# W_down's products of two groups added up in the same banks, sums spread over VectorE, single banks in the tail

## The chip, the cores and the metric

The kernel runs on one core of a Trainium2 chip. The time is that of the device in microseconds (us); what is compared is the median of several runs of the same program. A matmul here is of 128x128 against 128x512.

## The reference

One decoder layer on x of 1024 tokens by 1024 columns, float32. It has a mixer (two groups of heads), and then a multilayer perceptron between two norms:

```
x = x + rms_norm(mix @ w_out, norm_mix_post)
h = rms_norm(x, norm_ffn_pre)
f = square(relu(h @ w_up))              # 1024 x 4096
x = x + rms_norm(f @ w_down, norm_ffn_post)
```

The change lies in the perceptron, but for one small helper that also serves the norms of the mixer.

## The kernel before, in words

Every product is done in three matmuls: an operand is split into a high part (a cast on ScalarE) and a low part (the rest, a subtraction on another engine), and high x high, high x low and low x high are added in PSUM (`mm3`). `split(h, l, src, eng)` does it; without `eng` the low part goes to GpSimd.

Both products of the perceptron are done in a scheme of seven products in place of eight (after Strassen and Winograd): sums of quarters of h and of W are formed first, and seven products of such sums give the quarters of the result.

The stages in order: the mixer in two halves (to about 440 us), ordered by a scheduler that simulates the engines. Then the **early pairs** (`early_pair`, banks `pe`, 16 pairs of row blocks of W_up, to 548 us), with the sums of h's quarters (`raw12`, `raw22`, `raw_t3` and the split blocks t1 to t4) as one piece of code between pair 5 and pair 6. From here the order of TensorE is that of the code. Then the **pair loop** (banks `puB`, `puC`, `puD`, to 774 us), which writes squares and their sums to memory (`fsp`, `fpl`). Then **W_down** (banks `pd`): 7 groups, each with 7 products of 24 matmuls, and for each product a piece of f (`fr`, loaded, then split into `f0`, `f1`) and a piece of W (`wr` loaded, `wt` sums, split into `whd`, `wld`); each product is flushed by one add on VectorE into one of seven accumulators `acc1` to `acc7` of 128x2048. Group 7, the last, is done without the scheme in the **tail** (banks `pl`): 8 tiles of 128 tokens, two halves of 512 columns, 12 matmuls a half; VectorE adds the accumulator, ScalarE sums the squares, GpSimd multiplies by the norm's weight, VectorE computes the root in a chain of small instructions (`rstd_steps`) and finishes with one multiply and add, and the output is written.

Loads of W and f are issued on SyncE's queue, loads of W_up for the pair loop on ScalarE's. All instructions of the four engines are recorded by one helper (line 72), so lines don't tell them apart; the names of the tiles do.

## Time and profile before

| | us |
|---|---|
| median of 3 runs | 1132.75 (1127.96 to 1136.23) |
| the profiled execution | 1130.96 |
| its span | 1129.2 |
| TensorE busy, share of the span | 1043.9, 92% |
| VectorE | 814.9, 72% |
| ScalarE | 499.4, 44% |
| GpSimd | 446.0, 39% |

The span goes from the first to the last instruction of the profiled execution; its mean granted clock of TensorE is 0.974 of the full one. An engine's share is a mean over stages that have different limits, so that the stages are read one by one below.

### The profile page before, as it was taken

The page shows a single profiled execution, that of the slowest core. Times are in us where ns is not written, and L with a number is a line of the kernel's source. Part 1 is how long each engine was busy: PE and PEld are TensorE (multiplying, and loading weights), DVE is VectorE, ACT ScalarE, POOL GpSimd, SP SyncE. Part 2 cuts the span into 40 slices and gives each one's busy share as a digit, 9 for nine tenths or more (in the row PEclk, how much of TensorE's full clock was granted, in tenths as well). Part 3 has the DMA queues.
Part 4 walks back from the last instruction along what each step waited for, and adds up shares of the span by engine and source line. Part 5 has one row for each costly group of instructions (what it writes and reads, how often), then busy time and mean ns, then how long its engine had stood idle before and what let it go on. Part 6 is the DMA issues. An engine that isn't in the chain of part 4 may idle for free.

```text
span 1129.2 us, 13208 instructions
## 1 busy us (share of the span) xinstructions
PE 1043.9 (92%) x4735; PEld 843.7 (75%) x4735; DVE 814.9 (72%) x1273; ACT 499.4 (44%) x672; POOL 446.0 (39%) x214
## 2 busy tenths in 40 slices
PE   4998999999899999977999999998999999998885
PEld 3876787777688787766777888886888888886663
DVE  6547986369985737384467777776389889989787
ACT  4547454444635434644334444444743333332221
POOL 4453426324353433493011111113544444357833
PEclk9999999999899999988999999998999999999898
DMA  6434312327542225735767666773445434632132
GB/s 206 113 108 135 131 57 80 126 75 224 172 150 70 94 75 161 241 104 161 257 223 224 223 223 224 226 246 137 147 168 172 150 126 168 235 122 72 56 121 102
DMA packets 139657, 172.41 MB, mean 153 GB/s; under 512 B 8404, under 2 KB 83272, under 8 KB 139592
## 3 DMA queue, kind: packets, MB, share of 16 engines
q1 hardware_dynamic: 105160, 152.70, 40.8%
q10 hardware_dynamic: 34432, 18.88, 5.7%
...
## 4 chain that ended last, share of the span: by engine, by line
PE 63%; DVE 19%; DMA 6%; issue 5%; ACT 3%; POOL 2%; SPq 1%; DVEq 0%; ACTq 0%; POOLq 0%
PE pd L72 21%; PE pso L72 7%; PE puB L72 6%; PE puC L72 5%; PE pl L72 4%; PE pe L72 4%; PE puD L72 3%; DVE acc L72 3%; PE psz L72 2%; PE psv L72 2%; DVE gg L72 2%; DVE v L72 2%; DMA wu<-in_w_up_dram 2%; DVE rr L72 2%; DVE xg L72 2%
## 5 line engine op out<-in xcount | busy, mean ns | idle before, releaser
L72 POOL TENSOR_TENSOR wl<-ws,wh 128x1024 fp32r<-128x1024 f32 x72 | 180.0, 2506 | 237.8 <-ACT wh L72 237.7
L72 PE MATMUL pd<-whd,f 128*128 128x512 f32 x784 | 246.3, 395 | 9.8 <-DVE acc L72 5.4
L72 POOL TENSOR_TENSOR f<-fr,f 128x1024 fp32r<-128x1024 f32 x49 | 124.7, 2548 | 153.9 <-ACT f L72 153.7
L72 PEld LDWEIGHTS pd<-whd,f 128*128 128x128 f32 x784 | 149.5, 191 | 43.7 <-ACT whdl L72 5.7
L72 PE MATMUL pd<-wld,f 128*128 128x512 f32 x392 | 154.7, 395 | 0.0
L72 ACT CAST f<-fr 128x1024 fp32r<-128x1024 f32 x49 | 51.5, 1054 | 147.2 <-PE pd L72 123.6
L72 POOL TENSOR_TENSOR wlb<-sa,whb 128x1024 fp32r<-128x1024 f32 x16 | 38.4, 2401 | 186.8 <-ACT whb L72 154.1
L72 ACT CAST wh<-ws 128x1024 fp32r<-128x1024 f32 x72 | 75.4, 1047 | 75.2 <-issue 14.7
L72 DVE TENSOR_TENSOR acc<-pd,acc 128x2048 f32<-128x2048 f32 x41 | 93.7, 2286 | 15.9 <-PE pd L72 15.7
L72 PEld LDWEIGHTS pd<-wld,f 128*128 128x128 f32 x392 | 74.9, 191 | 15.6
L72 ACT ACTIVATE u<-u 128x512 f32<-128x512 f32 (+1 forms) x66 | 44.3, 672 | 62.4 <-DVE u L72 57.1
L72 DVE TENSOR_TENSOR wld<-wt,whd 128x1024 fp32r<-128x1024 f32 x28 | 56.6, 2026 | 16.2 <-ACT whd L72 16.2
L72 PE MATMUL pe<-hTh,wh 128*128 128x512 f32 x128 | 53.0, 414 | 15.2 <-ACT s1e L72 13.0
L72 PE MATMUL pe<-hTl,wh 128*128 128x512 f32 x128 | 51.9, 406 | 0.0
L72 PE MATMUL pe<-hTh,wl 128*128 128x512 f32 x128 | 51.7, 404 | 0.0
...
L72 DVE TENSOR_TENSOR wld<-wr,whd 128x1024 fp32r<-128x1024 f32 x21 | 40.5, 1929 | 9.8 <-ACT whd L72 9.7
L72 DVE TENSOR_SCALAR gg<-gg,acs 128x128 f32<-128x128 f32 x64 | 29.7, 523 | 21.4 <-DMA gg<-acd 21.4
L72 DVE TENSOR_TENSOR u<-puB,s 128x512 f32<-128x512 f32 x32 | 22.1, 691 | 30.7 <-DMA s<-early 19.6
L72 PEld LDWEIGHTS pe<-hTh,wh 128*128 128x128 f32 x128 | 25.3, 198 | 22.4 <-ACT s1e L72 14.1
L72 DVE TENSOR_TENSOR sa<-wu 128x512 f32<-128x512 f32 x16 | 11.1, 692 | 41.2 <-DMA wu<-in_w_up_dram 41.2
L72 PE MATMUL pl<-whdl,f0l 128*128 128x512 f32 x64 | 27.9, 436 | 13.0 <-DVE acc L72 13.0
...
## 6 DMA issues: line engine op xcount, KB each, us to landing
...
```

Source lines behind the costliest of these rows:

```text
L72: ins = fn(*a, **k)
```

## The change

Four things are done. The chain of a root, for one column, uses one-input instructions with two values from memory in place of two-input ones. The sums of h's quarters become a generator that the early pairs from the sixth on draw step by step, all of it on VectorE, and with it the low parts of the weights of these pairs. W_down takes its first six groups as (0), (1, 2), (3, 4), (5, 6): the products of two groups are added up in the same banks before one flush, product 2 goes on in the banks of product 1 after its flush, and 3 in those of 5; the order is 1, 5, 2, 3, 6, 7, 4; the final sums of accumulators all lie on VectorE. The raw tiles of W are cut in other pieces with a third buffer, and the first two pieces of f use the buffers of the weights of the pair loop. The tail has eight banks of 512 columns instead of two tiles of four banks; its tiles form pairs for the root, but for the last two; the rest of x is loaded in two pieces, and the steps of chains and finishes are drawn between adds.

```diff
         else:
-            dve.scalar_tensor_tensor(v, ss, 0.5 / n, base, op0=ALU.mult, op1=ALU.add)
+            dve.tensor_scalar(v, ss, 0.5 / n, base, op0=ALU.mult, op1=ALU.add)
         yield
         dve.tensor_scalar(ti, v.bitcast(I32), 1, None, op0=ALU.logical_shift_right)
         yield
@@ -152,12 +153,15 @@
         for _ in range(3):
             yield
             if w == 1:
-                dve.scalar_tensor_tensor(t, v, r, r, op0=ALU.mult, op1=ALU.mult)
+                dve.tensor_scalar(t, r, r, v, op0=ALU.mult, op1=ALU.mult)
             else:
                 dve.tensor_mul(t, v, r)
                 dve.tensor_mul(t, t, r)
             yield
-            dve.scalar_tensor_tensor(r, t, 1.5, r, op0=ALU.subtract, op1=ALU.mult)
+            if w == 1:
+                dve.tensor_scalar(r, t, 1.5, r, op0=ALU.subtract, op1=ALU.mult)
+            else:
+                dve.scalar_tensor_tensor(r, t, 1.5, r, op0=ALU.subtract, op1=ALU.mult)
...
-    def next_unit(ahead=2):
+    def next_unit(ahead=2, eng=None):
         i = state["use"]
         state["use"] += 1
         while state["load"] < min(i + 1 + ahead, len(units)):
-            load_unit()
+            load_unit(eng)
         return ready[i]
...
-        wh, wl = next_unit()
+        wh, wl = next_unit(2, dve if p >= N_TG else pool)
...
-    for hf in range(2):
-        cs = slice(hf * 256, (hf + 1) * 256)
-        r12, r22, r3 = raw12[:, :, cs], raw22[:, :, cs], raw_t3[:, :, cs]
-        hs = {k: (v[0][:, :, cs], v[1][:, :, cs]) for k, v in B.items()}
-        sub(pool, r3, r22, r12)
-        for y in hs["b11"]:
-            sub(dve, r12, r12, f(y))
-        sub(dve, r22, r22, r12)
-        split(*hs["t2"], r22, dve)
-        split(*hs["t1"], r12)
-        split(*hs["t3"], r3)
-        for y in hs["b21"]:
-            sub(dve, r22, r22, f(y))
-    B["t4"] = t8(fpool, "tmp", "t4h"), t8(tpool, "raw", "t4l", F32R, 2)
-    split(*B["t4"], raw22, dve)
+    def t_blocks():
+
+        for hf in range(2):
+            cs = slice(hf * 256, (hf + 1) * 256)
+            r12, r22, r3 = raw12[:, :, cs], raw22[:, :, cs], raw_t3[:, :, cs]
+            hs = {k: (v[0][:, :, cs], v[1][:, :, cs]) for k, v in B.items()}
+            sub(dve, r3, r22, r12)
+            sub(dve, r12, r12, f(hs["b11"][0]))
+            yield
+            sub(dve, r12, r12, f(hs["b11"][1]))
+            sub(dve, r22, r22, r12)
+            yield
+            split(*hs["t2"], r22, dve)
+            yield
+            split(*hs["t1"], r12, dve)
+            yield
+            split(*hs["t3"], r3, dve)
+            for y in hs["b21"]:
+                sub(dve, r22, r22, f(y))
+            yield
+        B["t4"] = t8(fpool, "tmp", "t4h"), t8(tpool, "raw", "t4l", F32R, 2)
+        split(*B["t4"], raw22, dve)
+
+    sums = t_blocks()
     for p in range(N_TG, N_PAIR):
+        next(sums, None)
         nxt = early_pair(p)
         rest()
         rest = nxt
+    for _ in sums:
+        pass
...
+    SG = [(0,), (1, 2), (3, 4), (5, 6), (last,)]
+    sg_of = {g: (n, gs.index(g)) for n, gs in enumerate(SG) for g in gs}
+    ORD = (1, 5, 2, 3, 6, 7, 4)
+    MORE = {2: 1, 3: 5}
...
+    def raw_tile(n):
+
+        if n not in raws:
+            tag = (hT_tag + ("wr",))[n % 3]
+            raws[n] = (hpool if n % 3 < 2 else dpool).tile([P, 8, 512], F32, tag=tag, bufs=1, name=f"wr{n}")
+        return raws[n]
+
+    def rows(g, h):
+        n, gi = sg_of[g]
+        return raw_tile(2 * n + h)[:, 4 * gi:4 * gi + 4, :].rearrange("p (r c) n -> p r c n", r=2)
+
+    def w_load(n, h, gs=None):
+        for g in gs or SG[n]:
+            for r in range(2):
+                d = nc.sync.dma_start(rows(g, h)[:, r], downs[4 * g + 2 * r + h][1])
+                wr_loads.append(d.ins.name)
...
-            t_ = dpool.tile([P, 2, 512], F32, tag="wt", bufs=3, name=f"w{key}_{g}")
+            t_ = a_ if key == "t4" else dpool.tile([P, 2, 512], F32, tag="wt", bufs=4, name=f"w{key}_{g}")
...
-        fh = f_piece(f"{g}_{i}")
+        fh = f_piece(f"{g}_{i}", None if len(pcs) < N_CARRY else ("fh", "fl"))
...
-    def flush(g, i, ps):
+    def flush(n, i, ps):
         a_ = accs
-        if g == 0:
+        if n == 0:
             act.copy(a_[i], ps)
-        elif g == last - 1 and i == 4:
+            return
+        if n == len(SG) - 2 and i == 4:
             sub(dve, a_[4], a_[4], ps)
-        else:
-            add(dve, a_[i], ps, a_[i])
-        if g < last - 1:
             return
-        if i == 1:
+        add(dve, a_[i], ps, a_[i])
+        if n < len(SG) - 2:
+            return
+        if i == 6:
             add(dve, a_[6], a_[6], a_[1])
-            add(pool, a_[2], a_[2], a_[1])
-        elif i == 6:
+            add(dve, a_[3], a_[3], a_[6])
+        elif i == 7:
             add(dve, a_[7], a_[7], a_[6])
-        elif i == 7:
-            sub(pool, a_[4], a_[7], a_[4])
-        elif i == 5:
-            add(dve, a_[6], a_[6], a_[5])
-            add(dve, a_[3], a_[3], a_[6])
-            add(pool, a_[7], a_[7], a_[5])
-
-    w_raw(0, (0, 2))
+            sub(dve, a_[4], a_[7], a_[4])
+            add(dve, a_[5], a_[5], a_[7])
...
-        ps = psum2.tile([P, 4, 512], F32, tag="pd", bufs=2, name=f"pd{g}_{i}")
+        if g == gs[0]:
+            banks[i] = banks[MORE[i]] if i in MORE else \
+                psum2.tile([P, 4, 512], F32, tag="pd", bufs=2, name=f"pd{n}_{i}")
+        ps = banks[i]
         for t in range(4):
             tsl = slice(t * P, (t + 1) * P)
             for q in range(2):
-                mm3(ps[:, t, :], fh[:, q, tsl], fl[:, q, tsl], h[:, q, :], l[:, q, :], q == 0, q == 1)
-        flush(g, i, ps)
-    for n in range(len(seq) + 2, len(preps)):
-        if n + 1 < len(preps):
-            floads[n + 1]()
-        preps[n]()
+                mm3(ps[:, t, :], fh[:, q, tsl], fl[:, q, tsl], h[:, q, :], l[:, q, :],
+                    g == gs[0] and q == 0 and i not in MORE, g == gs[-1] and q == 1,
+                    skip_group_check=i in MORE)
+        if g == gs[-1]:
+            flush(n, i, ps)
...
+    for t in range(8):
+        if t % 4 == 0:
+            xq4 = raw_tile(2 * len(SG) + t // 4)
+            after_w(nc.sync.dma_start(xq4.rearrange("p (t c) n -> p t (c n)", c=2),
+                                      x2d[t * P:(t + 4) * P, :].rearrange("(t p) d -> p t d", p=P)))
+        xqs.append(xq4[:, 2 * (t % 4):2 * (t % 4) + 2, :].rearrange("p c n -> p (c n)"))
     dve.held = True
-    for t in range(8):
-        xqs.append(now["tok"].tile([P, D], F32, tag="tok", bufs=4, name=f"xq{t}"))
-        after_w(nc.sync.dma_start(xqs[t], x2d[t * P:(t + 1) * P, :]))
-        ss = const.tile([P, 2], F32, tag="ss2", bufs=8, name=f"ssy{t}")
-        ps = psum2.tile([P, 4, 512], F32, tag="pd", bufs=2, name=f"pl{t}")
-        tsl = slice(t * P, (t + 1) * P)
-        for dh in range(2):
-            ds_ = slice(dh * 512, (dh + 1) * 512)
-            a_ = acc(t, dh)
-            if t and dh == 0:
-                advance(t - 1, 4)
-            for j in range(4):
-                mm3(ps[:, dh, :], ffs[j][0][:, tsl], ffs[j][1][:, tsl], us[j][0][:, dh, :],
-                    us[j][1][:, dh, :], j == 0, j == 3)
-            add(dve, a_, ps[:, dh, :], a_)
-            junk = now["tok"].tile([P, 512], BF16, tag="junk", bufs=1, name=f"yj{t}{dh}")
-            act.activation(junk, a_, AF.Square, accum_out=ss[:, dh:dh + 1])
-            pool.tensor_tensor(a_, a_, wfpost[:, ds_], op=ALU.mult)
-            if dh == 0:
-                if t:
-                    advance(t - 1, 9)
-                    finish(t - 1, 1)
-                base = rstd_base(ss[:, 0:1], D)
-            elif t:
-                finish(t - 1, 0)
-        steps.append(rstd_steps(ss[:, 1:2], D, base))
-        rs.append(next(steps[t]))
-    advance(7, 9)
-    finish(7, 0)
-    finish(7, 1)
+    for ts in TAIL:
+        ss = sss[ts] = const.tile([P, len(ts), 2], F32, tag=f"st{len(ts)}", bufs=4, name=f"ssy{ts[0]}")
+        for j, t in enumerate(ts):
+            tsl = slice(t * P, (t + 1) * P)
+            for dh in range(2):
+                ds_ = slice(dh * 512, (dh + 1) * 512)
+                a_ = acc(t, dh)
+                ps = psum3.tile([P, 512], F32, tag="pl", bufs=8, name=f"pl{t}{dh}")
+                for i in range(4):
+                    mm3(ps, ffs[i][0][:, tsl], ffs[i][1][:, tsl], us[i][0][:, dh, :],
+                        us[i][1][:, dh, :], i == 0, i == 3)
+                add(dve, a_, ps, a_)
+                junk = now["tok"].tile([P, 512], BF16, tag="junk", bufs=1, name=f"yj{t}{dh}")
+                act.activation(junk, a_, AF.Square, accum_out=ss[:, j, dh:dh + 1])
+                pool.tensor_tensor(a_, a_, wfpost[:, ds_], op=ALU.mult)
+                some(6 if len(ts) > 1 else 12)
+        todo.append(chain_op(ts))
+        for t in ts:
+            todo += [finish_op(t, 0), finish_op(t, 1)]
+    some(1000)
```

The order changes as follows. First VectorE at the early pairs, before: the sums of h's quarters (`raw12`, `raw22`, against the split blocks `hTh`, `hTl`) and the low part of t2, in one run.

```order
L72 TENSOR_TENSOR b22l_3496<-tg3_1_4202,b22h_3495 128x4x128
L72 TENSOR_TENSOR raw12_3497<-raw12_3497,hTh_105 128x4x256
L72 TENSOR_TENSOR raw12_3497<-raw12_3497,hTl_106 128x4x256
L72 TENSOR_TENSOR raw12_3497<-raw12_3497,hTh_105 128x4x256
L72 TENSOR_TENSOR raw22_3498<-raw22_3498,raw12_3497 128x4x256
L72 TENSOR_TENSOR raw12_3497<-raw12_3497,hTl_106 128x4x256
L72 TENSOR_TENSOR raw22_3498<-raw22_3498,raw12_3497 128x4x256
L72 TENSOR_TENSOR t2l_4217<-raw22_3498,t2h_4216 128x4x256
L72 TENSOR_TENSOR raw22_3498<-raw22_3498,hTh_105 128x4x256
L72 TENSOR_TENSOR t2l_4217<-raw22_3498,t2h_4216 128x4x256
L72 TENSOR_TENSOR raw22_3498<-raw22_3498,hTl_106 128x4x256
```

And now, at the same place, where `wl66` to `wl68` are low parts of the weights of early pairs:

```order
L73 TENSOR_TENSOR wl66_4308<-ws66_4305,wh66_4307 128x1024
L73 TENSOR_TENSOR raw_t3_4222<-raw22_3498,raw12_3497 128x4x256 x2
L73 TENSOR_TENSOR raw12_3497<-raw12_3497,hTh_105 128x4x256
L73 TENSOR_TENSOR t3l_4221<-raw_t3_4222,t3h_4220 128x4x256
L73 TENSOR_TENSOR raw12_3497<-raw12_3497,hTh_105 128x4x256
L73 TENSOR_TENSOR t3l_4221<-raw_t3_4222,t3h_4220 128x4x256
L73 TENSOR_TENSOR raw12_3497<-raw12_3497,hTl_106 128x4x256
L73 TENSOR_TENSOR wl67_4348<-ws67_4345,wh67_4347 128x1024
L73 TENSOR_TENSOR raw12_3497<-raw12_3497,hTl_106 128x4x256
L73 TENSOR_TENSOR raw22_3498<-raw22_3498,raw12_3497 128x4x256
L73 TENSOR_TENSOR t1l_4219<-raw12_3497,t1h_4218 128x4x256
L73 TENSOR_TENSOR wl68_4390<-ws68_4387,wh68_4389 128x1024
```

The weights' low parts and those of t3 and t1 are new on VectorE and stand between the sums, which come in other turns; GpSimd has no instruction between the last weight of the early pairs that it still splits and the first of the pair loop.

Then ScalarE at the entry into W_down, before: squares of the pair loop's last sums (`u2_15`, `u3_15`), and the cast of the first f piece, `f00_1`, behind them.

```order
L72 ACTIVATE f22_15_6408<-f22_15_6408 128x512 x2
L912 DMA fpl_3936<-f22_15_6408 128x512
L72 ACTIVATE u3_15_6407<-u3_15_6407 128x512 x2
L912 DMA fpl_3936<-u3_15_6407 128x512
L72 ACTIVATE u2_15_6365<-u2_15_6365 128x512 x2
L912 DMA fpl_3936<-u2_15_6365 128x512
L72 CAST f00_1_6484<-fr0_1_6478 128x1024
L72 CAST f00_2_6494<-fr0_2_6482 128x1024
```

And now the same cast, `whf0_1`, in a buffer of the weights:

```order
L73 CAST whd15_6346<-wu31_6281 128x512
L73 ACTIVATE u2_13_6135<-u2_13_6135 128x512 x2
L73 ACTIVATE f22_14_6304<-f22_14_6304 128x512 x2
L73 CAST whf0_1_6485<-fr0_1_6478 128x1024
L916 DMA fpl_3936<-f22_14_6304 128x512
L73 ACTIVATE u3_14_6303<-u3_14_6303 128x512 x2
L916 DMA fpl_3936<-u3_14_6303 128x512
L73 CAST whd0_1_6489<-wr0_6475 128x1024
L73 CAST whf0_5_6495<-fr0_5_6483 128x1024
L73 ACTIVATE u2_14_6250<-u2_14_6250 128x512 x2
```

It stands ahead of the squares of pair 14 and of all of pair 15.

Last VectorE at the end of W_down, before: flushes (`acc<-pd,acc`), sums of accumulators (`acc<-acc,acc`) and low parts of W (`wld`).

```order
L72 TENSOR_TENSOR acc7_6474<-acc7_6474,acc6_6473 128x2048
L72 TENSOR_TENSOR acc7_6474<-pd6_7_8188,acc7_6474 128x2048
L72 TENSOR_TENSOR wldl0_8295<-wr7_8173,whdl0_8294 128x1024
L72 TENSOR_TENSOR acc5_6472<-pd6_5_8225,acc5_6472 128x2048
L72 TENSOR_TENSOR wldl1_8331<-wr7_8173,whdl1_8330 128x1024
L72 TENSOR_TENSOR acc6_6473<-acc6_6473,acc5_6472 128x2048
L72 TENSOR_TENSOR acc2_6469<-pd6_2_8266,acc2_6469 128x2048
L72 TENSOR_TENSOR acc3_6470<-acc3_6470,acc6_6473 128x2048
L72 TENSOR_TENSOR wldl2_8367<-wr7_8173,whdl2_8366 128x1024
L72 TENSOR_TENSOR acc3_6470<-pd6_3_8302,acc3_6470 128x2048
L72 TENSOR_TENSOR wldl3_8375<-wr7_8173,whdl3_8374 128x1024
L72 TENSOR_TENSOR acc4_6471<-acc4_6471,pd6_4_8338 128x2048
```

And now:

```order
L73 TENSOR_TENSOR acc6_6473<-pd3_6_8095,acc6_6473 128x2048
L73 TENSOR_TENSOR wldl0_8240<-wr8_7868,whdl0_8239 128x1024
L73 TENSOR_TENSOR acc6_6473<-acc6_6473,acc1_6468 128x2048
L73 TENSOR_TENSOR acc3_6470<-acc3_6470,acc6_6473 128x2048
L73 TENSOR_TENSOR wldl1_8275<-wr9_8195,whdl1_8274 128x1024
L73 TENSOR_TENSOR acc7_6474<-pd3_7_8170,acc7_6474 128x2048
L73 TENSOR_TENSOR wldl2_8310<-wr8_7868,whdl2_8309 128x1024
L73 TENSOR_TENSOR acc7_6474<-acc7_6474,acc6_6473 128x2048
L73 TENSOR_TENSOR acc4_6471<-acc7_6474,acc4_6471 128x2048
L73 TENSOR_TENSOR acc5_6472<-acc5_6472,acc7_6474 128x2048
L73 TENSOR_TENSOR wldl3_8318<-wr9_8195,whdl3_8317 128x1024
L73 TENSOR_TENSOR acc4_6471<-acc4_6471,pd3_4_8247 128x2048
```

Five flushes stand in the rows before and three in those of now. Of the sums of accumulators four were on VectorE and three on GpSimd; now there are five, all on VectorE, three of them in a row ahead of the last low part of W and the last flush.

## Rows read from the trace of the kernel before

**Rows 1.** Busy time by stage: start:end, length, then each engine, clock, DMA.
```profile
core 0: us, PE busy (x) PEld busy (x) DVE busy (x) ACT busy (x) POOL busy (x), PEclk, DMA share, GB/s
28.00:484.00 456.00, 434.82 (x2158) 351.49 (x2157) 301.72 (x747) 225.66 (x327) 191.91 (x103) 0.98 0.40 126
484.00:525.00 41.00, 28.03 (x99) 22.04 (x99) 32.89 (x13) 19.33 (x26) 27.27 (x10) 0.83 0.37 117
498.30:501.00 2.70, 2.70 (x7) 2.12 (x8) 2.67 (x2) 1.44 (x2) 0.51 (x1) 0.50 0.69 215
525.00:548.00 23.00, 23.00 (x103) 19.07 (x102) 7.21 (x9) 9.86 (x16) 3.78 (x2) 1.00 0.51 165
548.00:600.00 52.00, 48.72 (x209) 38.61 (x208) 32.27 (x44) 21.41 (x30) 9.57 (x4) 1.00 0.76 255
600.00:774.00 174.00, 173.85 (x753) 140.88 (x752) 129.09 (x183) 82.19 (x114) 26.44 (x11) 1.00 0.68 220
774.00:790.00 16.00, 11.63 (x34) 8.50 (x34) 12.01 (x8) 7.64 (x9) 9.58 (x4) 0.68 0.46 157
790.00:1020.00 230.00, 230.00 (x1017) 190.50 (x1016) 191.54 (x102) 97.16 (x92) 104.91 (x43) 1.00 0.46 161
1020.00:1061.40 41.40, 31.78 (x130) 24.90 (x128) 41.19 (x15) 9.99 (x10) 35.54 (x9) 0.94 0.20 63
1061.40:1121.00 59.60, 50.55 (x192) 37.38 (x192) 43.52 (x102) 12.95 (x32) 24.09 (x17) 0.93 0.29 102
1121.00:1129.20 8.20, 0.00 (x0) 0.00 (x0) 4.73 (x13) 0.72 (x2) 1.26 (x1) 0.71 0.26 96
```
**Rows 2.** TensorE's timeline: start, length, instruction; in brackets the wait before.
```profile
498.22 0.80 PE L72 MATMUL pe<-hTh,wh 128*128 128x512 f32 x1 [6.99 <-ACT s1e L72]
...
517.76 0.79 PE L72 MATMUL pe<-hTh,wh 128*128 128x512 f32 x1 [5.99 <-ACT s1e L72]
...
777.66 0.79 PE L72 MATMUL pd<-whd,f 128*128 128x512 f32 x1 [3.55 <-ACT f L72]
...
1030.38 0.47 PE L72 MATMUL pd<-whd,f 128*128 128x512 f32 x1 [2.78 <-DVE acc L72]
...
1038.22 0.47 PE L72 MATMUL pd<-whd,f 128*128 128x512 f32 x1 [2.15 <-DVE acc L72]
...
1061.44 0.76 PE L72 MATMUL pl<-whdl,f0l 128*128 128x512 f32 x1 [4.22 <-DVE acc L72]
...
1073.89 0.50 PE L72 MATMUL pl<-whdl,f0l 128*128 128x512 f32 x1 [0.78 <-DVE acc L72]
```
**Rows 3.** The timelines of VectorE and GpSimd, early pairs.
```profile
485.55 6.70 POOL L72 TENSOR_TENSOR t3l<-raw_t,t3h 128x1024 fp32r<-128x1024 f32 x2
...
486.70 3.31 DVE L72 TENSOR_TENSOR raw<-raw,hTl 128x1024 f32<-128x1024 f32 x1
...
511.13 1.21 DVE L72 TENSOR_TENSOR raw<-raw,hTl 128x1024 f32<-128x1024 f32 x1
```
**Rows 4.** The timelines of VectorE and GpSimd at small and one-input instructions.
```profile
10.66 2.30 DVE L72 SCALAR_TENSOR_TENSOR rr<-rt,rr 128x1 f32<-128x1 f32 x1
...
111.22 3.06 DVE L72 TENSOR_SCALAR gg<-gg,acs 128x128 f32<-128x128 f32 x4
111.60 2.41 POOL L72 TENSOR_TENSOR wl<-ws,wh 128x1024 fp32r<-128x1024 f32 x1 [4.70 <-ACT wh L72]
...
455.83 5.18 POOL L72 TENSOR_TENSOR wl<-ws,wh 128x1024 fp32r<-128x1024 f32 x2 [10.15 <-ACT wh L72]
457.62 0.15 DVE L72 TENSOR_SCALAR rv<-ssg 128x1 f32<-128x1 f32 x1 [1.22 <-ACT ssg3j L72]
```
**Rows 5.** VectorE's sums of accumulators, from the page's groups and the timeline.
```profile
L72 DVE TENSOR_TENSOR acc<-pd,acc 128x2048 f32<-128x2048 f32 x41 | 93.7, 2286 | 15.9 <-PE pd L72 15.7
...
1044.66 4.49 DVE L72 TENSOR_TENSOR acc<-acc,acc 128x2048 f32<-128x2048 f32 x1
```
**Rows 6.** VectorE's timeline in the tail, two finishes.
```profile
1077.70 1.68 DVE L72 SCALAR_TENSOR_TENSOR acc<-acc,rr,xq 128x512 f32<-128x512 f32 x1
...
1121.45 0.74 DVE L72 SCALAR_TENSOR_TENSOR acc<-acc,rr,xq 128x512 f32<-128x512 f32 x1
```

More of the change, by code (lines that the diff above doesn't have):

```diff
@@ L1116, in f_piece @@
         fr = frs[name]
-        hl = tuple(dpool.tile([P, 2, 512], F32R, tag=t_, bufs=bufs, name=f"f{i}" + name)
-                   for i, t_ in enumerate(tags))
+        hl = piece([P, 2, 512], "f" + name) if tags is None else \
+            tuple(dpool.tile([P, 2, 512], F32R, tag=t_, bufs=bufs, name=f"f{i}" + name)
+                  for i, t_ in enumerate(tags))
         split(*hl, fr)
@@ L1133, in d_prep @@
         pcs[g, i] = fh, (h, l)
-    last = N_GROUP - 1
-    seq = [(g, i) for g in range(last) for i in ((1, 2, 3, 5, 6, 7, 4) if g < last - 1 else (1, 6, 7, 5, 2, 3, 4))]
+    seq = [(n, g, i) for n, gs in enumerate(SG[:-1]) for i in ORD for g in gs]
     us, ffs = [], []
@@ L1173, in hymba_kernel @@
-    w_raw(0, (0, 2))
-    floads[0]()
-    w_raw(0, (1, 3))
-    for n in range(2):
-        floads[n + 1]()
-        preps[n]()
-    for n, (g, i) in enumerate(seq):
-        if n % 7 == 2:
-            w_raw(g + 1)
-        floads[n + 3]()
-        preps[n + 2]()
+            sub(dve, a_[4], a_[7], a_[4])
+            add(dve, a_[5], a_[5], a_[7])
+    w_load(0, 0)
+    floads[0]()
+    w_load(0, 1)
+    for m in range(2):
+        floads[m + 1]()
+        preps[m]()
+    banks = {}
+    for m, (n, g, i) in enumerate(seq):
+        gs = SG[n]
+        k = m - seq.index((n, gs[0], ORD[0]))
+        if k == len(gs):
+            w_load(n + 1, 0)
+        elif k == 5 * len(gs) + 1:
+            w_load(n + 1, 1)
+        floads[m + 3]()
+        preps[m + 2]()
@@ L1241, in hymba_kernel, with some, chain_op, op @@
-    advance(7, 9)
-    finish(7, 0)
-    finish(7, 1)
+    todo = []
+    def some(k):
+        while k and todo:
+            if todo[0]() == "done":
+                todo.pop(0)
+            k -= 1
+    def chain_op(ts):
+        it = chain(ts)
+        def op():
+            try:
+                next(it)
+            except StopIteration:
+                return "done"
+        return op
+    def finish_op(t, dh):
+        def op():
+            finish(t, dh)
+            return "done"
+        return op
```

54 lines of the change are left out of this document (32 added, 22 removed).

## The prediction

> **What bounds the kernel now.** I read the table of stages first, then TensorE's waits in order of time, then the engines around each wait. In the table [rows 1] the reader is to compare TensorE's busy time with the length of each stage, and the granted clock beside it. [...] The stretch from 600 to 774 loses 174.00 - 173.85, nothing.
>
> So TensorE bounds the long middle, and the time to be had lies in five places. At four of them the waits [rows 2] say who ends them: ScalarE's copy s1e at 498.22 and 517.76 (6.99 and 5.99 us), ScalarE's cast of an f piece at 777.66 (3.55), VectorE's acc at 1030.38, 1038.22 and 1061.44 (2.78, 2.15, 4.22), and acc again at each tile of the tail (0.78). [...]
>
> **The change part by part.** *1. Sums over the early pairs.* Before, VectorE has a burst of two-input sums there. The row at 486.70 is one: 3.31 us for 128x1024 while GpSimd has two splits of the same shape, 6.70 us for both [rows 3]; the one at 511.13 has the same shape and takes 1.21 with GpSimd quiet. ScalarE's casts stand behind that burst, s1e behind the casts, and TensorE behind s1e. The change gives GpSimd's 14 instructions of the stretch (2 raw_t3, 2 t3l, 2 t1l, 8 weight splits) to VectorE, and GpSimd has nothing from the last plain weight split to the first split of the pair loop. VectorE then has 26 instructions of 1024 elements (18 sums and splits of t blocks, 8 weight splits) and t4l of 2048: 26 x 1.21 + 2 x 1.21 = 34 us, and the 7.2 us it has from 525 to 548 already. That is 41 in the 45.7 us that TensorE needs for its 99 + 103 matmuls. It fits, but not by much: two or three sums stand between two weight splits, 2.4 to 3.6 us beside a pair of 5.4, so a weight split comes in time. Of the 18.6 I take back 17.5, between 12 (a part of the second wait stays) and 18.6.
>
> *2. The pair loop's start.* Two MB of W_down instead of four are loaded there; the stage from 548 to 600 loses 52.0 - 209 x 0.2262 = 4.7, of which the four loads less may give 0 to 3. I take 1.
>
> *3. Into W_down.* Before, ScalarE casts the first f piece behind the last squares of the pair loop, and TensorE waits for it. Now the first two f pieces use buffers that exist before the loop ends, and their casts stand ahead of the squares of the last pairs. The next in line is the f piece of product 2, whose load is as it was. Of 8.3 I take 7, between 4 and 8.
>
> *4. Half the flushes.* Of 41 adds and one subtraction of 128x2048 on VectorE 21 are left. Inside 790 to 1020 this gains nothing: TensorE is busy there throughout, and what is hidden stays hidden. If VectorE's 191.54 us of 230 were the bound it would show. The cost is in what the two-group order needs: a piece of W and of f for two groups at once. In the first 38 us of the stage (7 products of 24 x 0.2262) about 9 MB have to come in (three loads of 2 MB and the f pieces); the chip moved 255 GB/s from 548 to 600, at which 9 MB take 35 us, and 220 from 600 to 774, 41 us. So a wait of 0 to 3; I charge 1.
>
> *5. The end of W_down.* The last products now end in another order, and the sums of whole accumulators stand behind flushes 6 and 7 alone. The waits at 1030.38 and 1038.22 and what is slow or late behind them are 12.0 - 4.2 = 7.8. VectorE has fewer flushes in front of them; a sum of accumulators costs 4.49 beside GpSimd [rows 5], three of them 13.5, and the last two products leave 21.8 us (each now takes 10.9 for two groups). I take 7 of it, between 3 and 8.
>
> *6. The tail.* The 4.22 at its start and 12 inside it come from a bank tile of 4 banks, of which two are in use at a time: a tile's first matmul waits for the add of the tile before last. With eight single banks TensorE can be four tiles ahead, so it is VectorE's sum of work that counts. For a pair of tiles: 4 adds and 4 finishes at about 0.74, a chain of 13 small ones at 0.15 to 0.2, about 8.2 us; and 0 to 3.8 more, if each of GpSimd's four products in that time holds up one instruction (a finish took 1.68 in the middle of the tail, 0.74 at its end, [rows 6]; 4 x 0.94). That is 8.2 to 12.0 against 10.9 of matmuls, so TensorE sets the pace by a little. At the start something new is late: the f pieces of the last group are split when the last products give their buffers back, about 7 us past the last product, and the third and fourth are needed 5 to 7 us into the tail: a wait of 0 to 5, I take 2, and 1.5 for slow matmuls behind it. Start to end: 43.4 + 2 + 1.5 + 8.2 + about 1 more at the end for chain and finishes = 56, where before it is 1129.2 - (1061.44 - 4.22) = 72. So 16, between 10 (VectorE sets the pace) and 20; I take 14.
>
> *7. The small chain of a root.* For width 1 its two-input instructions become one-input ones with values from memory. The row at 10.66 shows one of 128x1 that took 2.30 us [rows 4]. A one-input 128x1 at 457.62 took 0.15 with GpSimd busy from 455.83 for 5.18. But that one has constants, not values from memory; with such a value and 128x128, four took 3.06 at 111.22 while GpSimd held 2.41 from 111.60 on. So from 0 to 6 (three such waits ahead of the first products); nearest by shape is 457.62, and I take 2, as the loads of weights also stand before the first products. [...]
>
> *8. The front.* The scheduler permutes it: 199 of TensorE's instructions up to the early pairs move by more than ten places, none is added. TensorE loses 456.00 - 434.82 = 21 there in many small waits, so I cost the new order at nothing, with 6 either way.
>
> **Sum.** 17.5 + 1 + 7 - 1 + 7 + 14 + 2 = 47.5. The profiled execution took 1130.96 (span 1129.2), which is 1.8 below the median of the runs, 1132.75, a fifth of their spread of 8.3; I work from 1130.96 and get 1083.5, and say **1083**.
>
> **The rivals.** *A, VectorE's sums do not get cheaper* (this is the one that ends slower). If it is not GpSimd that makes a sum take 3.3, the 26 and t4l take 26 x 3.35 + 4.6 and the rest 7: 99 us in a stage that lasts 64 now. That is 1083 + 17.5 + 35 = 1136. It decides from 3.15 us a piece on (94 us for the stage, which eats all the other gains). Against it is 511.13 at 1.21. 0.03. *B, VectorE sets the pace of the tail and the last f pieces are late*: 12.0 a pair and a wait of 5: 1083 + 4 + 3 = 1090, with slow matmuls 1092; for it are the 43.52 us of VectorE in 59.6 now. 0.20. *C, W for two groups comes late*: the middle of the stage moves 161 GB/s; should that be what it gets, 9 MB take 56 us, 18 more: 1101. Against it is that 161 is only what was asked for. 0.08. *D, the new order of the front costs* 10: 1093. For it: nothing in the change orders that part, and a wait of some microseconds is easily made. 0.10. *E, the shared banks do not do what they say*, a product 2 waiting for the flush of product 1: product 5 lies between, 5.4 to 10.9 us, and a flush takes 2.29 (93.7 / 41, [rows 5]), so it is not to be expected; 3 groups x 2 waits of 2 us: 1095. 0.03.
>
> **How the numbers follow.** The forecast has 0.56, with its own range of 1073 to 1091 from the bounds of the parts. Eight in ten need B, D and most of C: 1069 to 1105. A measurement of this kernel can tell about 1% from no change (1122 to 1144): faster by more 0.95, within it 0.03 (A at 1136, and cases that lose nearly all), slower 0.02.
>
> **What would show it.** Part 1: sums at 1.2 on VectorE between the early pairs, no wait over 1 us for s1e, clock 1.00. Part 3: no wait over 1.5 at the first pd. Part 4: TensorE full as before, VectorE at some 60% in the middle. Part 5: no wait for acc before the first pl. Part 6: tiles of 5.4 instead of 6.6, and one short wait for an f piece. Part 7: no small instruction over 0.5 in the first 28 us. What would make it wrong: waits for wr or fr at the third product of W_down, or VectorE busy through the whole tail while TensorE is done.

## The result, and the profile after

The changed kernel takes **1085.68 us** (median of 4 runs, 1084.19 to 1087.13). The kernel before, on the same chip, takes 1132.94 (4 runs, 1127.96 to 1136.23). The ratio is 0.9586, 95% interval 0.9548 to 0.9625: 47 us less, where 1083 was forecast. The profiled execution took 1084.19, its span is 1082.5.

The page of the changed kernel, first the engines' totals, then the group of W_down's flushes (busy time, mean ns of one, and idle time of the engine ahead of them):

```profile
PE 1026.2 (95%) x4735; PEld 835.8 (77%) x4735; DVE 761.1 (70%) x1246; ACT 500.1 (46%) x673; POOL 389.0 (36%) x197
...
L73 DVE TENSOR_TENSOR acc<-pd,acc 128x2048 f32<-128x2048 f32 x20 | 45.7, 2287 | 10.1 <-PE pd L73 10.1
```

The flushes are 20 (and one subtraction) at 2.287 us, where there were 41 (and one subtraction) at 2.286 [rows 5]. To see where the time came from I cut both traces at the same events, the first and last matmul of each kind. The stages of the changed kernel by its table (start:end, length, TensorE's busy time and matmuls, weight loads, VectorE, ScalarE, GpSimd, clock, DMA):

```profile
160.00:200.00 40.00, 33.21 (x157) 27.22 (x155) 25.70 (x40) 14.98 (x20) 17.12 (x8) 0.87 0.26 72
...
435.90:526.80 90.90, 90.90 (x417) 75.32 (x416) 60.29 (x92) 57.13 (x89) 17.08 (x7) 1.00 0.64 204
526.80:748.75 221.95, 221.47 (x962) 180.16 (x960) 161.46 (x224) 104.34 (x144) 41.16 (x17) 1.00 0.71 228
...
748.75:1017.74 268.99, 267.30 (x1178) 220.87 (x1177) 202.90 (x104) 114.79 (x111) 123.08 (x49) 1.00 0.48 165
...
1017.70:1025.90 8.20, 1.86 (x10) 1.21 (x8) 8.14 (x4) 2.00 (x2) 5.49 (x2) 0.79 0.44 174
1025.90:1030.00 4.10, 4.10 (x11) 3.29 (x12) 0.00 (x0) 0.00 (x0) 0.70 (x1) 0.59 0.00 0
1030.00:1069.50 39.50, 39.48 (x175) 32.33 (x173) 28.51 (x66) 10.14 (x28) 17.97 (x14) 1.00 0.18 67
1069.50:1082.50 13.00, 0.00 (x0) 0.00 (x0) 8.33 (x26) 1.45 (x4) 3.41 (x3) 0.66 0.32 120
```

The reader is to see three full stages (busy time at most 1.7 us short of the length, clock 1.00), and two places that are not: 160 to 200, and both ends of the tail. Against the same events of the kernel before, in us:

| stage | before | after | gained | predicted |
|---|---|---|---|---|
| start to first matmul of the early pairs | 435.4 | 435.9 | -0.5 | 2 (parts 7, 8) |
| early pairs, to the first of the pair loop | 112.5 | 90.9 | 21.5 | 17.5 (part 1) |
| pair loop, to its last matmul | 226.2 | 222.1 | 4.1 | 1 (part 2) |
| from there to the last product of W_down's groups | 283.1 | 268.8 | 14.3 | 13 (parts 3, 4, 5) |
| tail | 72.0 | 64.8 | 7.2 | 14 (part 6) |
| sum | | | 46.7 | 47.5 |

The sum is right; four of its rows miss, two by 4.0 and 3.1 us too little and two by 6.8 and 2.5 us too much. Not every row can be read to a microsecond: in the kernels below, where the code of a stage is the same, the early pairs take 90.8 to 91.0 and the tail 64.6 to 64.9, but the first early pair starts at 433.1 to 437.2, the pair loop takes 221.9 to 224.8, and W_down up to its last product 268.8 to 270.5.

TensorE's timeline in the changed kernel answers [rows 2] (the wait ahead of an instruction is in brackets):

```profile
171.86 0.50 PE L73 MATMUL pso<-wh,mixbh 128*128 128x512 f32 x1 [2.89 <-DVE hTl L73]
...
756.55 0.50 PE L73 MATMUL pd<-wld,whf 128*128 128x512 f32 x1 [1.69 <-DVE wld L73]
...
1019.17 0.39 PE L73 MATMUL pl<-wldl,f0l 128*128 128x512 f32 x1
1025.89 0.80 PE L73 MATMUL pl<-whdl,f0l 128*128 128x512 f32 x1 [6.34 <-DVE acc L73]
```

The waits of 6.99 and 5.99 for s1e are gone, and those for an f piece (3.55) and for acc in W_down (2.78, 2.15) with them. A new one of 6.34 stands in the tail, behind the eighth matmul. Half a tile has twelve; in the order that the program got, the second half tile comes behind eight of the first, so that TensorE's order is not that of the code here. What it waits for, VectorE's and ScalarE's timelines there:

```profile
1011.48 8.88 DVE L73 TENSOR_TENSOR acc<-acc,acc 128x2048 f32<-128x2048 f32 x3
1020.29 3.36 DVE L73 TENSOR_TENSOR wldl<-wr,whdl 128x1024 fp32r<-128x1024 f32 x1
1023.57 2.27 DVE L73 TENSOR_TENSOR acc<-acc,pd 128x2048 f32<-128x2048 f32 x1
```
```profile
1023.12 1.04 ACT L73 CAST f0l<-frl 128x1024 fp32r<-128x1024 f32 x1 [4.47 <-DMA frl<-fpl]
```

Product 4 is the last to end, at 1017.7, and its flush (the row at 1023.57) comes 5.9 us later: VectorE has three sums of accumulators and a late weight split ahead of it, in the order of the code. The single banks of the tail are cut from the same memory as the two bank tiles of W_down, so the tail's second bank is free only when that flush has read product 4: it ends at 1025.84, the wait at 1025.89. Behind the wait the granted clock was 0.59 from 1025.90 to 1030.00, where 11 matmuls took 4.10 us, and 1.00 from there to the last matmul.

In the early pairs VectorE's rows answer [rows 3]:

```profile
484.61 1.22 DVE L73 TENSOR_TENSOR raw<-raw,hTl 128x1024 f32<-128x1024 f32 x1
485.75 1.22 DVE L73 TENSOR_TENSOR wl<-ws,wh 128x1024 fp32r<-128x1024 f32 x1
```

Every sum is at 1.22 (`raw`), with weight splits between them (`wl`). And at the end of the program, VectorE after the last matmul:

```profile
1072.74 1.41 DVE L73 SCALAR_TENSOR_TENSOR acc<-acc,rr,wr 128x512 f32<-128x512 f32 x2
1074.07 0.68 DVE L73 TENSOR_TENSOR acc<-pl,acc 128x512 f32<-128x512 f32 x1
```

The last add, of a product that TensorE had ended by 1069.5, runs at 1074.07, behind the whole root chain and the finishes of tile 6.

### The profile page after: what moved, and what is told of

Read it like the earlier page. It is cut to its first block, busy times and chain, and to the rows that moved or that the text cites. A ratio compares the mean times of both kernels' runs of the same rounds, so it can differ in the third digit from the quotient of the medians.

```text
span 1082.5 us, 13146 instructions
## 1 busy us (share of the span) xinstructions
PE 1026.2 (95%) x4735; PEld 835.8 (77%) x4735; DVE 761.1 (70%) x1246; ACT 500.1 (46%) x673; POOL 389.0 (36%) x197
## 4 chain that ended last, share of the span: by engine, by line
PE 71%; DVE 16%; DMA 4%; ACT 4%; issue 3%; SPq 1%; POOL 1%; DVEq 0%; ACTq 0%
PE pd L73 22%; PE pe L73 8%; PE puC L73 8%; PE puB L73 8%; PE pso L73 8%; PE puD L73 4%; PE pl L73 3%; DVE v L73 3%; PE psv L73 2%; PE psz L73 2%; DMA gg<-acd 2%; DVE acc L73 2%; DVE gg L73 1%; PE psB L73 1%; DVE rt L73 1%
## 5 line engine op out<-in xcount | busy, mean ns | idle before, releaser
L73 POOL TENSOR_TENSOR wl<-ws,wh 128x1024 fp32r<-128x1024 f32 x64 | 160.6, 2516 | 209.3 <-ACT wh L73 198.1
L73 PE MATMUL pd<-whd,f 128*128 128x512 f32 x752 | 231.5, 389 | 0.0
L73 POOL TENSOR_TENSOR f<-fr,f 128x1024 fp32r<-128x1024 f32 x47 | 117.7, 2507 | 143.2 <-ACT f L73 134.9
L73 PEld LDWEIGHTS pd<-whd,f 128*128 128x128 f32 x752 | 141.2, 188 | 29.1
L73 PE MATMUL pd<-wld,f 128*128 128x512 f32 x376 | 146.3, 389 | 0.0
L73 DVE TENSOR_TENSOR acc<-pd,acc 128x2048 f32<-128x2048 f32 x20 | 45.7, 2287 | 10.1 <-PE pd L73 10.1
L73 DVE TENSOR_SCALAR gg<-gg,acs 128x128 f32<-128x128 f32 x64 | 21.2, 389 | 22.3 <-DMA gg<-acd 22.3
L73 DVE TENSOR_TENSOR wlc<-sa,whc 128x1024 fp32r<-128x1024 f32 x16 | 29.4, 1835 | 6.1 <-ACT whc L73 6.1
L73 PE MATMUL pso<-wh,mixbh 128*128 128x512 f32 x64 | 28.0, 438 | 4.2 <-DVE hTl L73 2.9
L73 ACT ACTIVATE f<-f 128x512 f32<-128x512 f32 x32 | 20.2, 633 | 25.0 <-DVE f L73 24.5
```

What stands on the lines that cost most here:

```text
L73: ins = fn(*a, **k)
```

## The experiments

Edits are against the changed kernel unless said otherwise. The ratios are to the kernel before, run on the same chip (medians 1130.11 to 1131.37).

**The tail.** The first experiment takes two of the three sums away from in front of product 4's flush.

```diff
-            sub(dve, a_[4], a_[4], ps)
+            add(dve, a_[4], ps, a_[4])
-            sub(dve, a_[4], a_[7], a_[4])
-            add(dve, a_[5], a_[5], a_[7])
+                if t == 2 and dh == 0:
+                    sub(dve, accs[4], accs[7], accs[4])
+                if t == 3 and dh == 0:
+                    add(dve, accs[5], accs[5], accs[7])
```

> The flush of product 4 no longer has two sums of accumulators in front of it (they go behind the fourth half tile of the tail). Theory (the 6.3 us wait at the second half tile is for product 4's banks, which VectorE reads last): the wait falls to the 2 to 3 us that the last f pieces are late, the tail is 4 us shorter, 1081 to 1083. Rival (the wait is for the last two f pieces, as the prediction had it): the wait stays near 6 and the time at 1085 to 1087.

It took 1081.33, ratio 0.9561 (0.9539 to 0.9582). TensorE's wait and the two parts of the tail, in its timeline and its table:

```profile
1020.80 0.50 PE L73 MATMUL pl<-whdl,f0l 128*128 128x512 f32 x1 [0.57 <-DVE acc L73]
```
```profile
1018.40:1063.20 44.80, 44.14 (x193) 35.53 (x191) 34.94 (x61) 11.40 (x28) 23.98 (x15) 1.00 0.21 81
1063.20:1080.40 17.20, 0.01 (x1) 0.00 (x0) 12.39 (x34) 2.17 (x6) 4.08 (x3) 0.62 0.33 122
```

The wait is down to 0.57 and TensorE's part of the tail is 44.8 where it was 51.8: the bank was the reason. But what follows the last matmul is 17.2 instead of 13.0. VectorE's work was only put off, and 4 of the 7 us came back; the tail is 62.0 instead of 64.8. The second experiment tests what the prediction had named instead, late f pieces: the third f piece goes into buffers that are free earlier, and the second load of x stands behind the f loads.

```diff
-                         (f_piece(f"l{i}") if i < 3 else f_piece(f"l{i}", ("wt", "wt"), 4))))
+                         (f_piece(f"l{i}") if i < 2 else f_piece(f"l{i}", ("wt", "wt"), 4))))
...
+            if t:
+                tc.add_manual_dep(d.ins, fr_loads[-1], order, reason="order")
```

> The third f piece of the last group gets buffers that are free earlier, and the 2 MB load of the second half of x goes behind the load of the fourth f piece. Theory (banks): the f pieces are there 3 to 5 us earlier and nothing comes of it, the wait for VectorE stays at 5 to 6.5 us, 1084 to 1087. Rival (f pieces): the wait falls to 2 or less, 1081 to 1082.

1085.84, ratio 0.9600 (0.9575 to 0.9624): nothing gained. TensorE's waits in its tail:

```profile
1020.66 0.50 PE L73 MATMUL pl<-whdl,f1l 128*128 128x512 f32 x1 [0.92 <-POOL f1l L73]
...
1026.09 0.79 PE L73 MATMUL pl<-wldl,f0l 128*128 128x512 f32 x1 [4.68 <-DVE wldl L73]
...
1028.29 0.80 PE L73 MATMUL pl<-whdl,f0l 128*128 128x512 f32 x1 [1.41 <-DVE acc L73]
```
```profile
1011.68 11.08 DVE L73 TENSOR_TENSOR acc<-acc,acc 128x2048 f32<-128x2048 f32 x3
```

The waits add up to 7.0, and the long one is for VectorE's weight split. So the f pieces did not hold TensorE at the tail's start. This is no clean test of what they cost, though: with the third piece in its new place VectorE's three sums (the row below TensorE's waits) take 11.08 instead of 8.88, so VectorE comes later. The third puts the roots of tiles 6 and 7 into one chain:

```diff
-    TAIL = ((0, 1), (2, 3), (4, 5), (6,), (7,))
+    TAIL = ((0, 1), (2, 3), (4, 5), (6, 7))
```

> The last two token tiles share one chain for the root, so that the chain and finishes of tile 6 no longer stand between the last two adds. Theory (the 13.0 us between the last matmul and the end are VectorE's queue, 4.9 us of it for tile 6's chain and finishes): 10 to 11 us, the time 2 to 3 shorter, 1083. Rival (the end is set by GpSimd's products and the writes of the output): 12.5 to 13.5 us, 1085 to 1086.

1085.79, ratio 0.9597 (0.9580 to 0.9615). The part after the last matmul is 11.9 instead of 13.0, between the theory and its rival, and the tail is 63.4; the whole did not move, and a gain of 1 us would not be seen in runs that differ by more than that. The three edits together:

> The three edits of the tail together. Theory (two things in a row at the tail's start, banks and then f pieces, and VectorE's queue at the end): the start loses 1 to 2 us instead of 6.3, the end takes 10 to 11 instead of 13.0, 1077 to 1079. Rival (one of the two at the start is nothing): 1079 to 1082.

**1079.90**, ratio 0.9556 (0.9529 to 0.9583), the lowest median of all the kernels here, though not clear of the first experiment's (1081.33). It is 6 us below the second and third experiment, but its runs (1079.11 to 1084.80) touch theirs (1084.16 to 1087.48). From the last product of the groups to the end it takes 59.0, where the changed kernel takes 64.8 and the first experiment 62.0. In these two traces the f pieces do count. GpSimd's split of the fourth f piece in the first experiment, VectorE's first sum of the tail there, and the same sum here:

```profile
1025.09 2.40 POOL L73 TENSOR_TENSOR f1l<-frl,f0l 128x1024 fp32r<-128x1024 f32 x1 [3.29 <-ACT f0l L73]
```
```profile
1028.11 1.89 DVE L73 TENSOR_TENSOR acc<-pl,acc 128x512 f32<-128x512 f32 x3 [7.36 <-PE pl L73]
```
```profile
1025.82 1.29 DVE L73 TENSOR_TENSOR acc<-pl,acc 128x512 f32<-128x512 f32 x2 [5.14 <-PE pl L73]
```

In the first experiment no half tile is complete before the fourth piece is split, at 1027.49; TensorE goes on with other half tiles, but VectorE stands idle for 7.36 us. With the pieces earlier its first sum starts 7.5 us behind the last product instead of 9.7. The forecast for the end did not hold: TensorE loses 0.8 at the start, as the theory said, but 14.2 us follow the last matmul, not 10 to 11, and the time is the rival's. The fourth kernel's table by stretch of the tail, and a piece of VectorE's and GpSimd's timelines:

```profile
1030.00:1045.00 15.00, 15.00 (x68) 12.43 (x67) 13.94 (x24) 2.90 (x8) 6.63 (x5) 1.00 0.10 36
1045.00:1063.20 18.20, 18.18 (x81) 14.73 (x79) 16.72 (x39) 5.07 (x14) 10.20 (x8) 1.00 0.23 86
1063.20:1078.00 14.80, 0.00 (x0) 0.00 (x0) 9.81 (x23) 1.45 (x4) 3.08 (x3) 0.61 0.38 142
```
```profile
1046.66 1.17 DVE L73 TENSOR_SCALAR rv<-tv 128x2 f32<-128x2 f32 x1
1047.86 1.22 DVE L73 TENSOR_SCALAR rti<-rv 128x2 int32<-128x2 int32 x1
1049.11 0.17 DVE L73 TENSOR_SCALAR rr<-rti 128x2 int32<-128x2 int32 x1
```
```profile
1046.51 2.54 POOL L73 TENSOR_TENSOR acc<-acc,wfpost 128x512 f32<-128x512 f32 x2 [0.34 <-ACT yj L73]
```

VectorE is busy 30.7 of 33.2 us while TensorE still works, and has 9.8 us left over when it is done: the end of the tail is VectorE's. The two small instructions at 1046.66 and 1047.86 end at 1047.83 and 1049.08, the second with GpSimd's pair (1049.05); the same kind takes 0.17 right behind. So I took six finishes off VectorE and gave them to ScalarE and GpSimd (an edit of the fourth kernel):

```diff
-        dve.scalar_tensor_tensor(a_, a_, rs[t], xqs[t][:, ds_], op0=ALU.mult, op1=ALU.add)
+        if dh and t < 6:
+            act.activation(a_, a_, AF.Copy, scale=rs[t])
+            pool.tensor_tensor(a_, a_, xqs[t][:, ds_], op=ALU.add)
+        else:
+            dve.scalar_tensor_tensor(a_, a_, rs[t], xqs[t][:, ds_], op0=ALU.mult, op1=ALU.add)
```

> The kernel with the three edits of the tail, and six of its finishes (the second halves of tiles 0 to 5) as a scaling on ScalarE and an addition on GpSimd. Theory (VectorE's work sets the pace of that tail): 4 to 5 us less on VectorE, of which 1 to 3 arrive, 1077 to 1079. Rival (GpSimd's six more instructions hold VectorE up for as long): 1080 to 1083.

1081.15, ratio 0.9553 (0.9533 to 0.9573), no different from the fourth: the tail is 59.0 again, as the rival had it, and VectorE is busy for 44.9 us of it, where it was 44.7 with six finishes more. What VectorE is spared comes back in longer instructions beside GpSimd, whose additions are new there (two of them took 5.04 us from 1043.71 on, beside the sum). One sum and one finish of VectorE's timeline:

```profile
1044.22 3.38 DVE L73 TENSOR_TENSOR acc<-acc,acc 128x2048 f32<-128x2048 f32 x1
...
1055.91 1.60 DVE L73 SCALAR_TENSOR_TENSOR acc<-acc,rr,wr 128x512 f32<-128x512 f32 x1
```

A finish alone takes 0.74 [rows 6], and the same 128x2048 sum took 2.28 in the fourth kernel.

**The early pairs.** Two things were changed there: which engine, and in what order. First the order alone is undone: all sums on VectorE, but held in one run ahead of the pairs.

```diff
+    dve.held = True
+    for _ in sums:
+        pass
...
+    dve.held, dve.last = False, None
```

> The sums of h's quarters are held together on VectorE ahead of the weight splits of pairs 6 to 15 (all still on VectorE, at 1.2 us each: 24 us in one run). Theory A (two causes before: GpSimd's lock and the one run, each worth about half): the early pairs take 100 to 106 us instead of 91, the time is 1095 to 1101. Theory B (only the lock counted, the run is short enough at 1.2 us): 91 to 94, 1085 to 1089.

GpSimd's lock is a name there for what [rows 3] show, a sum at 3.31 beside GpSimd's splits and at 1.21 without them. It took 1113.39, ratio 0.9856 (0.9825 to 0.9886), worse than I expected. Its timeline:

```profile
508.23 0.79 PE L73 MATMUL pe<-hTh,wl 128*128 128x512 f32 x1 [25.90 <-DVE wl L73]
```

The sums are at 1.22 here too, but the weight splits queue behind all of them: the stage takes 118.6, more than before the change (112.5), where the splits of that stretch were GpSimd's and did not stand behind VectorE's sums. Cheap sums in the wrong place are worth less than nothing. Then the engine alone is undone (14 instructions back on GpSimd):

```diff
-        wh, wl = next_unit(2, dve if p >= N_TG else pool)
+        wh, wl = next_unit()
-            sub(dve, r3, r22, r12)
+            sub(pool, r3, r22, r12)
-            split(*hs["t1"], r12, dve)
+            split(*hs["t1"], r12)
-            split(*hs["t3"], r3, dve)
+            split(*hs["t3"], r3)
```

> The sums stay a generator over the early pairs in the code, but GpSimd has its 14 instructions back. Theory A: sums at 3.3 us on VectorE where they meet GpSimd's, the early pairs take 100 to 113 us, 1095 to 1107. Theory C (spreading over the pairs was all): 91 to 95, 1085 to 1090.

1099.58, ratio 0.9730 (0.9702 to 0.9758). VectorE, GpSimd and TensorE in it:

```profile
478.50 3.42 DVE L73 TENSOR_TENSOR raw<-raw,hTh 128x1024 f32<-128x1024 f32 x1 [7.56 <-POOL raw_t L73]
```
```profile
476.07 4.76 POOL L73 TENSOR_TENSOR raw_t<-raw,raw 128x1024 f32<-128x1024 f32 x2
480.80 3.38 POOL L73 TENSOR_TENSOR t3l<-raw_t,t3h 128x1024 fp32r<-128x1024 f32 x1
```
```profile
499.75 0.80 PE L73 MATMUL pe<-hTh,wh 128*128 128x512 f32 x1 [7.12 <-ACT s1e L73]
...
514.61 0.50 PE L73 MATMUL pe<-hTh,wh 128*128 128x512 f32 x1 [1.22 <-ACT s1e L73]
```

The sums are at 3.4 again and the long wait for s1e is back; the stage takes 103.6, 12.7 more than with the change. That is less than the 21.5 that the stage gained, so something else has a part in it. It also undoes more than the engine: with the weight splits on GpSimd nothing stands between VectorE's sums, which run in one piece again (478.50 to 509.99). A kernel with GpSimd's work beside sums that are truly spread was not made, so engine and order are not fully told apart.

**The small chain.** The change with the old two-input chain:

```diff
-            dve.tensor_scalar(v, ss, 0.5 / n, base, op0=ALU.mult, op1=ALU.add)
+            dve.scalar_tensor_tensor(v, ss, 0.5 / n, base, op0=ALU.mult, op1=ALU.add)
-                dve.tensor_scalar(t, r, r, v, op0=ALU.mult, op1=ALU.mult)
+                dve.scalar_tensor_tensor(t, v, r, r, op0=ALU.mult, op1=ALU.mult)
...
```

> The change with the chain of a root as before, two-input instructions also for one column. Theory P (the chain gains 5 us up to the first psz product, and the new order of the front that comes with it loses as much between 160 and 200 us): the first psz at 80 to 82 instead of 75.7, the first early pair at 434 to 438 all the same, 1084 to 1088. Rival Q (what is lost there has nothing to do with the chain): the first early pair at 440 to 442, 1090 to 1093.

1090.72, ratio 0.9641 (0.9620 to 0.9662). P's account of the front held (first psz at 82.5, first early pair at 437.0), its time did not. The early pairs take 94.0 instead of 90.9, and the tail 66.3 instead of 64.8. TensorE waits in the early pairs for copies that ScalarE makes of finished banks, three times; the changed kernel has none of these waits. Two of them:

```profile
450.44 0.50 PE L73 MATMUL pe<-hTh,wh 128*128 128x512 f32 x1 [0.51 <-ACT e L73]
...
457.46 0.50 PE L73 MATMUL pe<-hTh,wh 128*128 128x512 f32 x1 [1.29 <-ACT e L73]
```

And the reverse, the kernel before with the new chain and nothing else:

> The kernel before with the new chain alone. Theory P: the first psz at 75 to 77 instead of 80.9, the first early pair at 433 to 438 as before (435.4), no change in the time, 1128 to 1133. Rival Q: the first early pair at 429 to 431, 1123 to 1127.

1122.23, ratio 0.9925 (0.9907 to 0.9943). P's account of the front held (the first early pair starts at 435.57, before the change at 435.43), but its time did not: the kernel is 9 us faster, and not by Q's mechanism either. The early pairs take 103.8 there, 8.6 less, and the tail, whose roots are the same chain, 69.0 instead of 72.0; the pair loop takes 230.0 instead of 226.2. TensorE's waits in the early pairs:

```profile
501.78 0.79 PE L72 MATMUL pe<-hTh,wh 128*128 128x512 f32 x1 [7.09 <-ACT s1e L72]
...
516.63 0.50 PE L72 MATMUL pe<-hTh,wh 128*128 128x512 f32 x1 [1.33 <-ACT s1e L72]
```

The first wait stays, the second fell from 5.99 to 1.33, and two waits for e that the kernel before has earlier in the stage (0.57 and 1.64) are gone. These five kernels make a table of the early pairs' length:

| | old chain | new chain |
|---|---|---|
| GpSimd has the 14 instructions | 112.5 (before) | 103.8 (before with the new chain), 103.6 (change with GpSimd) |
| VectorE has them, spread | 94.0 | 90.9 (after) |

Moving the sums gives 18.5 with the old chain and 13 with the new one; the chain gives 8.6 alone and 3 beside the moved sums. The two overlap, since both take away the second wait for s1e. In the kernel before, four instructions of the chains, between 435.07 and 458.72, took 2.3 to 2.4 each in the first part of the early pairs, and in the one with the new chain none there takes over 0.45 for two. That this, through the scheduler's order on ScalarE, is what shortens the waits for e and the second wait for s1e, was not taken apart further.

**W_down.** All groups singly again:

```diff
-    SG = [(0,), (1, 2), (3, 4), (5, 6), (last,)]
+    SG = [(g,) for g in range(N_GROUP)]
```

> W_down's groups one by one again (42 flushes in place of 21), all else as in the change, products 2 and 3 still in the banks of 1 and 5. Theory (TensorE bounds the middle, the half of the flushes that went was hidden): W_down takes 269 us as in the change, within 2; 1084 to 1088, or 1 to 3 less for fewer bytes asked for at the start. Rival (part of the 14 us that the stage from the pair loop's end to the tail gained came from fewer flushes): 274 to 280 us, 1091 to 1097.

1093.11, ratio 0.9666 (0.9643 to 0.9689). Its table from the first product to the last, and then up to the tail's wait, and that wait:

```profile
745.99:1016.58 270.59, 268.91 (x1177) 221.58 (x1175) 229.61 (x123) 114.88 (x111) 123.52 (x49) 0.99 0.48 165
1016.58:1031.20 14.62, 0.00 (x0) 0.00 (x0) 14.53 (x6) 1.95 (x2) 6.34 (x2) 0.62 0.20 78
```
```profile
1031.29 0.77 PE L73 MATMUL pl<-whdl,f0l 128*128 128x512 f32 x1 [14.71 <-DVE acc L73]
```

VectorE has 229.6 us of work there instead of 202.9, and the stage is 270.6 instead of 269.0. The 1.6 is no price of the flushes: a wait of 1.7 is there in both, and in the first 20 us of the stage TensorE does 73 matmuls at a granted clock of 0.91 here and 80 at 1.00 in the changed kernel, but also 73 at 0.91 in the second and third experiment, which have the two-group order and take 270.4. In the middle the flushes are hidden. So the theory held for the stage and missed the time, as it had not looked at the tail: VectorE comes late to it, by 14.53 us of work that keeps the bank. The bank is another one than before: with single groups the last product lies in the other of the two bank tiles, and TensorE waits ahead of the tail's first matmul, not behind its eighth. With the late sums of the first experiment added:

> Groups one by one, with the last two sums of accumulators behind the fourth half tile of the tail. Theory (the two-group order is worth something only because it leaves VectorE time for its sums ahead of the tail): the wait at the tail's second half tile falls from 14.7 us to 4 to 7, of which half comes back at the end, 1086 to 1090. Rival (the wait with single groups is for pieces of W or f): it stays over 10, 1091 to 1094.

1090.39, ratio 0.9636 (0.9611 to 0.9660):

```profile
1027.92 0.76 PE L73 MATMUL pl<-whdl,f0l 128*128 128x512 f32 x1 [8.04 <-DVE acc L73]
```

The wait of 14.71 is down to 8.04, more than expected to be left, and the time is just above the theory's range. Against the first experiment (1081.33) the two-group order is worth 9 us, 7.7 of it in the tail (69.7 against 62.0); the rest lies in W_down, where it is within the scatter. Up to 1.8 of the 7.7, eight matmuls, may come from the other bank and not from VectorE's time. Last, the f pieces that are carried over from the pair loop:

```diff
-N_CARRY = 2
+N_CARRY = 0
```

> The first two f pieces of W_down use the buffers they had before. Theory (the cast's place in ScalarE's queue made the wait at the entry): the wait at the first product is back, 3 to 4 us and slow matmuls behind it, 5 to 7 in all; 1090 to 1093. Rival (the entry gained by the loads that no longer crowd there): 0 to 2; 1085 to 1088.

1091.16, ratio 0.9650 (0.9615 to 0.9685). TensorE's timeline at the first product:

```profile
749.62 0.50 PE L73 MATMUL pd<-whd,f 128*128 128x512 f32 x1 [3.55 <-ACT f L73]
```

The wait of 3.55 is back as it was [rows 2], and from the end of the pair loop to the last product it is 275.5 instead of 268.8: 6.7, or 5.1 against the kernels that take 270.4 there.

## Why the prediction was right, and where it was not

The parts start from what a stage loses, its length less its matmuls at 0.2262 us, which is what one took from 790 to 1020 (230.00 us for 1017, [rows 1]): 18.6 of 41.0 from 484 to 525 (99 matmuls), 8.3 of 16.0 from 774 to 790 (34), 12.0 of 41.4 from 1020 to 1061.4 (130), and 16.2 of 59.6 from there to 1121 (192).

**Part 1, right, and a little small.** Sums at 1.22, no wait over 0.5 us, clock 1.00, as said. 18.5 is what the move is worth with the old chain, against 17.5 predicted. The other 3 of the 21.5 are the chain's, by the waits for e, which the prediction had not looked for there. That both GpSimd's share and the place of the weight splits count is shown; how the 18.5 divides between them is not.

**Part 2, mis-sized.** 4.1 against 1, above its bound of 3. Of the 4.7 that the stage's start lost, nearly all went: the loop has 221.47 busy of 221.95. In other kernels with the same loop it takes up to 224.8, so the gain is 1.4 to 4.3. No experiment took this part alone, so whether it is the loads that are missing or the pairs ahead that are on time stays open.

**Part 3, right.** 5.1 to 6.7 by experiment, 7 predicted.

**Part 4, right in the middle, its worth put in the wrong place.** The half of the flushes that is gone changes nothing in the middle. No W or f piece was late but for one wait of 1.69, for the low part of a W piece, where 1 was charged. What the two-group order brings, 7 to 9 us, is VectorE's time at the end of W_down, and it shows in the tail. The waits for acc that part 5 takes back stay away from W_down with single groups too, so those 7 belong to the new order of products and sums, not to fewer flushes. W_down as a whole came to 14.3 against 13.

**Part 6, the step that failed.** "TensorE sets the pace by a little" and "a wait of 0 to 5, I take 2" for f pieces. The wait was 6.34, and for a bank: I had followed the new tiles' banks among each other and not asked whose memory the first ones inherit. The 1.5 for slow matmuls behind it was about right: 11 matmuls took 4.10 us at a granted clock of 0.59, 1.6 more than 11 x 0.2262; in [rows 1] the 7 behind the wait at 498.22 took 2.70 at 0.50, 1.1 more. With that wait out of the way (the first and the fourth experiment) VectorE sets the pace, as rival B had it, and ends 14 to 17 us behind the last matmul; in the changed kernel it is 13.0 where 9.2 was predicted. The tail gave 7.2 instead of 14, below the bound of 10. Rival B's 7 us for the tail is about what was missed (6.8), by another route: its late f pieces did not hold TensorE, but they keep VectorE idle at the tail's start once the bank is free. One reading was wrong without harm: the loss inside the tail before is 16.2, as worked out above; the 12 of part 6 takes off the 4.22, which lies ahead of that stretch. Its sum goes from start to end and does not use the 12.

**Parts 7 and 8, no gain at the front.** The chain does what was predicted of it. VectorE and GpSimd in the changed kernel, at the place of [rows 4]:

```profile
10.64 0.27 DVE L73 TENSOR_SCALAR rt<-rr,rv 128x1 f32<-128x1 f32 x1
```
```profile
10.59 2.35 POOL L73 TENSOR_TENSOR wl<-ws,wh 128x1024 fp32r<-128x1024 f32 x1 [8.82 <-ACT wh L73]
```

0.27 beside GpSimd, where the two-input form took 2.30. The first large products start 5.2 us earlier (75.65 against 80.89). But from 160 to 200 us it is given back. The kernel before in that stretch:

```profile
160.00:200.00 40.00, 37.85 (x200) 31.93 (x199) 27.44 (x62) 17.86 (x26) 18.67 (x8) 1.00 0.25 67
```

157 matmuls now, 200 then, with the 2.89 for hTl at 171.86 the first of two longer waits. The front ends at 435.9 as it did. The kernel before with only the new chain has the same wait of 2.89 and ends the front at 435.6, and the change with the old chain has 200 matmuls in that stretch again, so it is the order that comes with the new chain. Which row of the order makes hTl late was not tried. The gain of 2 at the front was wrong, and the same edit paid 3 to 8.6 us in the early pairs and 1.5 to 3 in the tail.

So the forecast came out right partly by luck, with errors that cancel: 7 too little in parts 1 and 2, and 9 too much in parts 6 to 8.
